# RWKV time mixing: inputs split once into two parts, wider weight splits, unmasked key products, factors padded to 112 rows

## The chip, the cores and the metric

One Trainium2 chip, of which the kernel uses one core. The core has TensorE (PE, with its weight loads shown apart as PEld), VectorE (DVE), ScalarE (ACT), GpSimd (POOL), SyncE (SP, which here only issues transfers) and 16 DMA engines. The metric is the device time of one execution in microseconds; the median of several runs counts.

## The reference

Two layers of a bidirectional encoder trunk, 256 tokens, width 2048, float32, one batch. Layer 0 is a Hyena/GLA block and an MLP, layer 1 an RWKV-7 block and an MLP; each sub-block has an adaLN in front and a gated residual behind. The change lies in the RWKV block alone:

```python
def rwkv7_block(h, mu, w_r, w_k, w_v, w0, w1, w2, a0, a1, a2, g1, g2, k_k, k_a, r_k, gn_g, gn_b, w_o):
    xx = 0.5 * (hp[:, :-2] + hp[:, 2:]) - h
    xr, xw, xk, xv, xa, xg = [h + xx * mu[j] for j in range(6)]
    r, k, v = heads(xr @ w_r), heads(xk @ w_k), heads(xv @ w_v)
    g = jax.nn.sigmoid(xg @ g1) @ g2
    kk = k * k_k;  kk = kk * rsqrt(max(sum(kk * kk), 1e-24))
    for d in range(2):                              # forwards and backwards
        logw = -0.606531 * sigmoid(w0[d] + tanh(xw @ w1[d]) @ w2[d])
        a = sigmoid(a0[d] + (xa @ a1[d]) @ a2[d])
        k_d = k * (1.0 + (a - 1.0) * k_a)
        # scan over time, per head (64 x 64 state):
        #   state = state * w_t + (state @ -kk_t) (kk_t * a_t)^T + v_t k_t^T;  o_t = state @ r_t
        state_out += o_d
        bonus += sum(r * k_d * r_k) * v
    o = groupnorm(state_out) * gn_g + gn_b + bonus
    return (o * g) @ w_o
```

The kernel does the scan in chunks of 64 tokens. Per head and chunk it needs the products of the decayed keys with each other, a 64x64 matrix `N`, and the inverse of a unit triangular matrix built from its strictly lower part.

## The kernel before

All large products are made of three TensorE products: each float32 operand is split into a high part (a cast to the type fp32r, on ACT) and a low part (the operand less its high part), and hi·hi, hi·lo and lo·hi are added up (`prod`, lines 502 to 507). The split itself is `split`, line 465: a cast on ACT (L466) and a subtraction on DVE, or on POOL where that engine is named (both L467).

The RWKV block (label `tm`, function `rwkv`) runs in these stages.

The **mixing stage**: the normalized input `h` and its difference `xx` are in SBUF. `spill_mixes` (L1275) forms xk, xr and xv, two of 16 feature tiles at a time, as float32 and writes them to the DRAM tensors `mix2`, `mix0` and `mix3`. `lora` (L1284) beside it makes the low-rank inputs. The first key products run woven into this.

The **keys stage**: four groups `n` of eight heads. For each, `rwkv_linear` (L1021) streams k, then r: eight tiles of weights of 128x1024 (512 KB) and eight input tiles `xu` (256 KB) read back from DRAM. `stream` (L994) prepares one tile ahead: it loads `xu` (two buffers), splits it with ACT and POOL into `xh` and `xl`, loads the next weights and splits the present ones in two halves of 512 columns (`split_weights`, with `fine` 2 from the constants `W1`, `W2`), ACT for `wh`, DVE for `wl`. So each of the four groups of each of the three products loads and splits the same input anew: 96 tiles. Woven between is `rwkv_keys` (L1326) for each of 16 pairs of heads `p`, twice (`d`, the direction): it takes LoRA factors `up` (97 rows: 96 and a bias; one load of 97x1024 for two pairs, L1180), forms decays, exponentials and the tile `ab` (DVE, L1374 to L1377), the products `N` in PSUM (L1387), multiplies them with the mask `nm` on their way to SBUF (DVE, L1393) and stores `ab` and `N` to DRAM. `invert` (L1405) of the group before runs beside it: long rows of small DVE steps (L1421, L1422), which read the strictly lower triangle only.

The **values stage** and the **output product**: `pair_load`, `pair_prep`, `pair_chain` and `pair_tail` for each pair, woven with the v products of the groups 1 to 3 (through `stream` again) and the output product `rwkv_out`.

What sets the order: `weave` deals out steps of these generators in given proportions, and a scheduler with a timeline model then orders each engine's instructions; every engine works through its own row in order. All loads and stores of the RWKV block except three go through SP's single row. In the program a transfer also waits until the one eight before it, which had the same completion semaphore, has landed. The last third of the kernel, the second MLP, follows when the output product is done.

Of the kernel before, what the change touches and what calls it, by code (L numbers as in the profile page):

```python
# [9 lines left out]
F32 = mybir.dt.float32  # L10
F32R = mybir.dt.float32r
# [97 lines left out]
def _rwkv_constants():  # L109
    o = {}  # L110
    for d in range(2):
        st = _block_tri(64, True, d == 1)
        inc = _block_tri(64, False, d == 1)
        o[f"cum{d}"] = np.concatenate([st, inc], axis=1) * np.float32(-0.606531)
        st64, inc64 = st[:64, :64], inc[:64, :64]
        z = np.zeros((64, 64), np.float32)
        top = np.concatenate([z, inc64], axis=1)
        bot = np.concatenate([st64, inc64], axis=1)
        o[f"mm{d}"] = np.concatenate([bot, top] if d else [top, bot], axis=0)
    lower = np.tril(np.ones((64, 64), np.float32), -1)  # L120
    o["nm"] = np.concatenate([lower, lower], axis=0)
    h = np.arange(P) // 64
    o["bo"] = (h[:, None] == h[None, :]).astype(np.float32)
    return o


def layout(i):
# [56 lines left out]
    for n, v in _rwkv_constants().items():  # L184
        (rk1 if n[:3] in ("cum", "nm") else rk).add(n, v)
    a["rc"], a["rc1"] = rk.array(), rk1.array()
# [28 lines left out]
class Build:  # L215
# [21 lines left out]
    def run(self):  # L237
# [3 lines left out]
        self.due, self.rate, self.turn, self.hold, self.starting = 0.0, 0.0, 0, None, False  # L241
        self.cut = None
        self.small = self.pool(ctx, "small", bufs=2)
# [221 lines left out]
    def split(self, a, hi, lo, eng=None):  # L465
        self.nc.scalar.copy(hi, a)  # L466
        d = (eng or self.nc.vector).tensor_tensor(lo, a, hi, ALU.subtract)  # L467
# [20 lines left out]
    def load(self, name, n, i, pools):  # L488

        self.turn += 1  # L490
        w = self.t(pools[self.turn % len(pools)], [P, 2, NB], "w")
        self.dma = self.nc.sync.dma_start(w, self.A[name][n, i // 2][:, i % 2 * 2 : i % 2 * 2 + 2]).ins
        self.tick(self.rate / 2)
        return w
# [487 lines left out]

    def open_linear(self, st, bufs, fine, finex):
        self.fine, self.finex = fine, finex
        self.ws = self.pool(st, self.name("ws"), bufs=bufs, reuse_waits="tile")
# [8 lines left out]
    def stream(self, name, n, src, tiles):  # L994

        nc = self.nc
        w = [self.load(name, n, 0, [self.wp])]

        def ahead(i):
            u = self.t(self.xt, [P, 2, T], "xu", bufs=2)  # L1000
            nc.sync.dma_start(u, src[:, 2 * i : 2 * i + 2, :])
            x = [self.t(self.xt, [P, 2, T], t, dt=F32R) for t in ("xh", "xl")]
            for j in range(self.finex):
                c = slice(j * T // self.finex, (j + 1) * T // self.finex)
                self.split(u[:, :, c], *(a[:, :, c] for a in x), nc.gpsimd)
# [8 lines left out]
        for i in range(tiles // 2):  # L1014
# [3 lines left out]
            for k in range(2):  # L1018
                yield 2 * i + k, [a[:, k, :] for a in x], [a[:, k, :] for a in v]

# [79 lines left out]
    def rwkv(self):  # L1100
# [12 lines left out]
        with ExitStack() as st:  # L1113
# [35 lines left out]
            with ExitStack() as st2:  # L1149
# [11 lines left out]
                self.xstack.close()  # L1161
                self.rate = 0.0
                mixes = self.spill_mixes(h, xx)
# [5 lines left out]
            with st1:  # L1169
                p1 = self.pool(st1, "p1", reuse_waits="tile")  # L1170
                for n in range(4):
# [3 lines left out]
                    def lane(o):  # L1175
                        for i in range(2):
                            p = 4 * n + 2 * i + o
                            if o == 0:
                                up[i] = self.t(p1, [97, 4, T], "up", bufs=2)
                                nc.sync.dma_start(up[i], A["rw_up"][p // 2])  # L1180
# [9 lines left out]
            with ExitStack() as st1:  # L1190
                self.open_linear(st1, 2, W2, X2)
                p2 = self.pool(st1, "p2", reuse_waits="tile")
# [68 lines left out]
                for n in range(4):  # L1261
# [9 lines left out]
                    self.residual("tm", n, pts[n])  # L1271
        self.open_gate()
# [53 lines left out]
    def rwkv_keys(self, rp, p, r, k, kk, kh, up):  # L1326
# [11 lines left out]
        for d in range(2):  # L1338
# [16 lines left out]
            Gp.tensor_tensor(u[1 - d], sc, k, ALU.mult)
# [4 lines left out]
            en = self.t(rp, [P, T], "en", bufs=3)  # L1360
            pt = self.pt([P, 2, 2, P])
# [12 lines left out]
            V.tensor_tensor(ar[:, 0, :], ar[:, 0, :], kk, ALU.mult)  # L1374
            for n in range(2):
                V.tensor_tensor(bk[:, :, n, :], c4(u[n]), c4(en), ALU.mult)
            V.tensor_tensor(ar[:, 1, :], ar[:, 1, :], r, ALU.mult)  # L1377
# [14 lines left out]
            for hd in range(2):  # L1392
                V.tensor_tensor(nt[:, hd], pts[hd], self.rc("nm").unsqueeze(1).to_broadcast([P, 2, 64]), ALU.mult)  # L1393
            nc.sync.dma_start(self.nd[b][:, d, 256 * pb : 256 * pb + 256], nt.rearrange("p h t j -> p (h t j)"))
# [319 lines left out]
```

## Time and profile before

| | us |
|---|---|
| median of 3 runs (range) | 3164.84 (3163.99 to 3170.43) |
| the profiled execution, its own time | 3173.39 |
| its span, first to last instruction | 3171.6 |
| PE busy | 2904.6 (92%) |
| DVE busy | 2195.9 (69%) |
| ACT busy | 1340.4 (42%) |
| POOL busy | 620.7 (20%) |
| mean granted TensorE clock | 0.96 |

The strip of the page cuts the span in 40 slices of 79 us; each digit is a busy share in tenths:

```profile
PE   5999899999999999979577777999998999999998
DVE  7899776657777787787368685975556677555554
PEclk9999999999999999999788897998999999999999
```

Slices 18 to 30 are the RWKV block. Read a time on the page with two things in mind. Matmuls are pipelined, so that the durations of a group add up to more than the stretch in which they ran; the busy time of a stretch counts overlaps once. And an idle engine costs only where the work that ends last hangs on it: a wait is to be followed to what ended it.

### The profile page before, as it was taken

The numbers are of one execution on the slowest core, as the hardware profiler recorded it, in microseconds if no ns is written. First come the engines' busy times: TensorE is split into PE (matmuls) and PEld (weight loads), VectorE is DVE, ScalarE is ACT, GpSimd is POOL, SyncE is SP. The second block draws the span as 40 slices with busy tenths as digits, with TensorE's granted clock in tenths as the row PEclk, the third lists the DMA queues.
The fourth block names the chain that finished last, engine by engine and source line by source line (L and its number), as shares of the span: only waits on it lengthen the run. The fifth ranks groups of instructions, "written<-read, shape, count | busy, mean of one in ns | idle before, by whom it ended". The sixth has DMA issues, their size and how long they took to land. (4 is left out here: it accounts for less than half of the span.)

```text
span 3171.6 us, 52610 instructions
## 1 busy us (share of the span) xinstructions
PE 2904.6 (92%) x20308; PEld 2513.1 (79%) x20308; DVE 2195.9 (69%) x3350; ACT 1340.4 (42%) x2083; POOL 620.7 (20%) x646
## 2 busy tenths in 40 slices
PE   5999899999999999979577777999998999999998
PEld 2677776799988998868476676787777998899986
DVE  7899776657777787787368685975556677555554
ACT  3233444444433444433354553444445444344443
POOL 1211100021100110023355464442323110001100
PEclk9999999999999999999788897998999999999999
DMA  9978777648889888966455567896635678555552
GB/s 320 326 257 290 245 269 265 230 150 285 291 305 314 291 295 301 311 214 226 152 185 175 178 208 192 270 292 208 192 108 192 224 250 284 196 188 180 199 193 99
DMA packets 285494, 741.39 MB, mean 234 GB/s; under 512 B 73601, under 2 KB 100097, under 8 KB 284092
## 3 DMA queue, kind: packets, MB, share of 16 engines
q1 hardware_dynamic: 284668, 734.40, 69.0%
q8 instruction: 159, 2.61, 0.3%
q10 hardware_dynamic: 576, 3.64, 0.3%
q14 instruction: 91, 0.75, 0.1%
HBM read 697.23 MB, written 40.70 MB: 233 GB/s over the span
## 5 line engine op out<-in xcount | busy, mean ns | idle before, releaser
L467 DVE TENSOR_TENSOR f_wl<-f_w,f_wh 128x1024 fp32r<-128x1024 f32 x512 | 631.0, 1233 | 444.5 <-ACT f_wh L466 440.4
L466 ACT CAST f_wh<-f_w 128x1024 fp32r<-128x1024 f32 x512 | 538.4, 1052 | 748.3 <-PE f_mm L507 319.3
L506 PE MATMUL f_mm<-f_h,f_wh 128*128 128x256 f32 x2048 | 579.6, 283 | 0.0
L505 PE MATMUL f_mm<-f_h,f_wh 128*128 128x256 f32 x2048 | 579.4, 283 | 0.0
L507 PE MATMUL f_mm<-f_h,f_wl 128*128 128x256 f32 x2048 | 579.0, 283 | 0.0
L506 PE MATMUL f_mm<-f_wl,f_hid 128*128 128x512 f32 x1024 | 398.6, 389 | 0.6 <-DVE f_wl L467 0.6
L507 PE MATMUL f_mm<-f_wh,f_hid 128*128 128x512 f32 x1024 | 398.5, 389 | 0.0
L506 PEld LDWEIGHTS f_mm<-f_h,f_wh 128*128 128x128 f32 x2048 | 393.2, 192 | 0.2
L505 PEld LDWEIGHTS f_mm<-f_h,f_wh 128*128 128x128 f32 x2048 | 393.0, 192 | 0.1
L507 PEld LDWEIGHTS f_mm<-f_h,f_wl 128*128 128x128 f32 x2048 | 392.9, 192 | 0.0
L505 PE MATMUL f_mm<-f_wh,f_hid 128*128 128x512 f32 x1024 | 357.9, 389 | 0.0
L467 POOL TENSOR_TENSOR f_hid<-f_u,f_hid 128x512 fp32r<-128x512 f32 x64 | 98.0, 1531 | 990.0 <-ACT f_hid L466 985.2
L467 DVE TENSOR_TENSOR tm_wl<-tm_w,tm_wh 128x512 fp32r<-128x512 f32 x256 | 206.0, 830 | 99.0 <-ACT tm_wh L466 98.4
L363 DVE SCALAR_TENSOR_TENSOR mix_w<-mix_w,mix_s 128x1024 f32<-128x1024 f32 x175 | 219.8, 1265 | 73.3 <-DMA mix_w<-in_ada_f 49.1
L505 PE MATMUL tm_mm<-tm_xh,tm_wh 128*128 128x256 f32 x768 | 242.9, 320 | 18.5 <-ACT tm_xh L466 11.1
L506 PE MATMUL tm_mm<-tm_xl,tm_wh 128*128 128x256 f32 x768 | 234.5, 306 | 8.8 <-POOL tm_xl L467 8.8
L363 DVE SCALAR_TENSOR_TENSOR f_w<-f_w,mix_s 128x1024 f32<-128x1024 f32 x174 | 233.4, 1344 | 2.3 <-DMA f_w<-in_ada_f 2.3
L507 PE MATMUL tm_mm<-tm_xh,tm_wl 128*128 128x256 f32 x768 | 232.6, 305 | 1.4 <-DVE tm_wl L467 1.4
L467 POOL TENSOR_TENSOR tm_xl<-tm_xu,tm_xh 128x512 fp32r<-128x512 f32 x113 | 169.4, 1500 | 310.5 <-ACT tm_xh L466 268.8
L506 PEld LDWEIGHTS f_mm<-f_wl,f_hid 128*128 128x128 f32 x1024 | 192.2, 188 | 40.9 <-DVE f_wl L467 1.2
L507 PEld LDWEIGHTS f_mm<-f_wh,f_hid 128*128 128x128 f32 x1024 | 192.2, 188 | 39.8
L505 PEld LDWEIGHTS f_mm<-f_wh,f_hid 128*128 128x128 f32 x1024 | 192.3, 188 | 39.7
(445 smaller groups left out, 5413.9 us busy)
## 6 DMA issues: line engine op xcount, KB each, us to landing
f_w<-in_w SPq DMA_DIRECT2D x512, 512.0 KB, 4.9
f_w<-in_ada_f SPq DMA_DIRECT2D x125, 512.0 KB, 5.5
mix_w<-in_ada_mix SPq DMA_DIRECT2D x96, 512.0 KB, 6.4
mix_w<-in_w_in SPq DMA_DIRECT2D x80, 512.0 KB, 5.2
mix_w<-in_ada_f SPq DMA_DIRECT2D x64, 512.0 KB, 5.0
f_w<-in_ada_tm SPq DMA_DIRECT2D x49, 512.0 KB, 5.7
tm_xu<-mix SPq DMA_DIRECT2D x96, 256.0 KB, 4.8
mix_w<-in_w_out SPq DMA_DIRECT2D x32, 512.0 KB, 4.7
```

The source lines that it names most:

```text
L363: V.scalar_tensor_tensor(w, w, 1.0, self.s[:, j * (D // 2) : (j + 1) * (D // 2)], ALU.mult, ALU.mult, accum_out=a[:, j, i : i + 1])
L466: self.nc.scalar.copy(hi, a)
L467: d = (eng or self.nc.vector).tensor_tensor(lo, a, hi, ALU.subtract)
L505: mm(out, lhsT=l[0], rhs=r[0], start=start, stop=False)
L506: mm(out, lhsT=l[0], rhs=r[1], start=False, stop=False)
L507: mm(out, lhsT=l[1], rhs=r[0], start=False, stop=stop)
```

## The change

- `spill_mixes` splits each mixed tile at once, with ACT and POOL: 24 splits for 96. The parts of xk stay in SBUF, in two tiles `xk` of 128x8x2x256 in fp32r. The parts of xr and xv go to DRAM as one tensor each, 512 KB per two feature tiles (16 stores of 512 KB for 24 of 256 KB), through two buffers `xs`.
- `stream` takes a slice of `xk` for the keys, and for r and v loads both parts in one transfer straight to the matmuls' operand (64 loads of 512 KB for 96 of 256 KB; three buffers). It loads weights three tiles ahead (`PF`).
- `W1` and `W2` go from 2 to 1: a weight tile is split by one cast and one subtraction of 1024 columns.
- `N` is copied from PSUM by ACT and no longer masked by DVE; the mask leaves the constants. The triangle that is read later is the same.
- The two DVE products of `bk` become one of 128x512, with `u` as one tile; `th` and `en` have two buffers for three.
- `rw_up` gets 15 rows of zeros, 112 in all; the matmuls use 97 as before.
- `wq` and `casts` are new names for another queue of weights; `wq` is None throughout, so nothing runs through them.

```diff
-W1, W2, X1, X2 = 2, 2, 1, 1
+W1, W2 = 1, 1
-PK = 8
+PK, PF = 8, 3
...
-    a["rw_up"] = np.stack(up, axis=1).reshape(97, 4, 8, T).transpose(2, 0, 1, 3)
+    up = np.stack(up, axis=1).reshape(97, 4, 8, T).transpose(2, 0, 1, 3)
+    a["rw_up"] = np.concatenate([up, np.zeros((8, 15, 4, T), np.float32)], axis=1)
...
     def stream(self, name, n, src, tiles):
         nc = self.nc
-        w = [self.load(name, n, 0, [self.wp])]
+        w = [self.load(name, n, i, [self.wp]) for i in range(PF)]
         def ahead(i):
-            u = self.t(self.xt, [P, 2, T], "xu", bufs=2)
-            nc.sync.dma_start(u, src[:, 2 * i : 2 * i + 2, :])
-            x = [self.t(self.xt, [P, 2, T], t, dt=F32R) for t in ("xh", "xl")]
-            for j in range(self.finex):
-                c = slice(j * T // self.finex, (j + 1) * T // self.finex)
-                self.split(u[:, :, c], *(a[:, :, c] for a in x), nc.gpsimd)
-            if 2 * i + 2 < tiles:
-                w.append(self.load(name, n, i + 1, [self.wp]))
+            if isinstance(src, list):
+                x = src[i // 4][:, 2 * i % 8 : 2 * i % 8 + 2]
+            else:
+                x = self.t(self.xt, [P, 2, 2, T], "x", bufs=self.xb, dt=F32R)
+                nc.sync.dma_start(x.bitcast(F32), src[:, 2 * i : 2 * i + 2])
+            if 2 * (i + PF) < tiles:
+                w.append(self.load(name, n, i + PF, [self.wp]))
             v = [self.t(self.ws, [P, 2, NB], t, dt=F32R) for t in ("wh", "wl")]
             self.split_weights(w[i], v)
             return x, v
...
-        self.xd = {j: tc.dram_tile([P, KT, T], F32, name=f"mix{j}") for j in (0, 2, 3)}
+        self.xd = {j: tc.dram_tile([P, KT, 2, T], F32, name=f"mix{j}") for j in (0, 3)}
...
+            xk = self.pool(st1, "xk", reuse_waits="tile")
+            self.xd[2] = [self.t(xk, [P, 8, 2, T], f"xk{i}", dt=F32R) for i in range(2)]
...
     def spill_mixes(self, h, xx):
...
-                self.nc.sync.dma_start(self.xd[j][:, k : k + 2, :], u)
+                if j == 2:
+                    x = self.xd[2][k // 8][:, k % 8 : k % 8 + 2]
+                else:
+                    x = self.t(self.hp, [P, 2, 2, T], "xs", bufs=2, dt=F32R)
+                self.split(u, x[:, :, 0], x[:, :, 1], self.nc.gpsimd)
+                if j != 2:
+                    self.nc.sync.dma_start(self.xd[j][:, k : k + 2], x.bitcast(F32))
...
-                                up[i] = self.t(p1, [97, 4, T], "up", bufs=2)
+                                up[i] = self.t(p1, [112, 4, T], "up", bufs=2)
...
-            for n in range(2):
-                V.tensor_tensor(bk[:, :, n, :], c4(u[n]), c4(en), ALU.mult)
+            V.tensor_tensor(bk, u.rearrange("p n (c t) -> p c n t", t=64), c4(en).unsqueeze(2).to_broadcast([P, 4, 2, 64]), ALU.mult)
...
-                V.tensor_tensor(nt[:, hd], pts[hd], self.rc("nm").unsqueeze(1).to_broadcast([P, 2, 64]), ALU.mult)
+                S.copy(nt[:, hd], pts[hd])
```

Every engine's order up to the RWKV block is the one of before. Three places within it follow, first as before, then as changed.

SP's row around the fourth load of factors, in group 1 of the keys stage (`xu` and `x` are inputs read back from `mix`, `w` weights, `E` the input of the inversion, `N` and `ab` stores of the keys):

```order
846 L1394 DMA nd_11803<-tm_N_13713 128x256
847 L1001 DMA tm_xu_13880<-mix_11783 128x512
848 L1180 DMA tm_up_14625<-in_rw_up 97x1024
849 L1001 DMA tm_xu_13994<-mix_11784 128x512
850 L1413 DMA tm_E_14020<-nd_11803 16x32x32 x4
851 L492 DMA tm_w_14266<-in_rw_k 128x1024
852 L1001 DMA tm_xu_14077<-mix_11784 128x512
853 L1402 DMA ab_11789<-tm_bon_13519 128x264
854 L1394 DMA nd_11803<-tm_N_13936 128x256
```

```order
819 L1009 DMA tm_x_13704<-mix_11783 128x1024
820 L494 DMA tm_w_13810<-in_rw_k 128x1024
821 L494 DMA tm_w_13884<-in_rw_k 128x1024
822 L1406 DMA nd_11802<-tm_N_13559 128x256
823 L1186 DMA tm_up_14365<-in_rw_up 112x1024
824 L1009 DMA tm_x_14140<-mix_11783 128x1024
825 L1425 DMA tm_E_13828<-nd_11802 16x32x32 x4
826 L494 DMA tm_w_13923<-in_rw_k 128x1024
```

Before, each weight tile has an `xu` load beside it, the keys' too. In the change the `x` loads here belong to r; the keys' stream has weights only, and they are issued three tiles ahead.

ACT's row in the keys stage (`wh`, `xh` are casts, `sig`, `th`, `sc`, `ab`, `en` steps of `rwkv_keys`):

```order
836 L466 CAST tm_wh_14385<-tm_w_14375 128x512 x2
837 L466 CAST tm_xh_14379<-tm_xu_14377 128x512
838 L1364 ACTIVATE tm_ab_14360<-tm_ps_14362 128x2x2x128
839 L1365 ACTIVATE tm_en_14361<-tm_ps_14362 128x256
840 L466 CAST tm_wh_14428<-tm_w_14333 128x512 x2
841 L466 CAST tm_xh_14424<-tm_xu_14422 128x512
842 L1343 ACTIVATE tm_sig_14406<-tm_ps_14407 128x256
```

```order
820 L465 CAST tm_wh_13925<-tm_w_13672 128x1024
821 L1377 ACTIVATE tm_ab_13876<-tm_ps_13878 128x2x2x128
822 L1378 ACTIVATE tm_en_13877<-tm_ps_13878 128x256
823 L465 CAST tm_wh_13999<-tm_w_13810 128x1024
824 L1356 ACTIVATE tm_sig_13948<-tm_mm_13949 128x256
825 L1361 ACTIVATE tm_th_13954<-tm_ps_13955 128x256
826 L1363 ACTIVATE tm_sc_13958<-tm_th_13954,tm_ksc_11818 128x256
827 L465 CAST tm_wh_14040<-tm_w_13884 128x1024
828 L1405 COPY tm_N_13975<-tm_ps_13976 128x128
829 L1405 COPY tm_N_13975<-tm_ps_13981 128x128
```

The casts of inputs are gone from the stage, a weight tile has one cast, and the copies of `N` stand among them.

DVE's row in the keys stage (`z` and `T` are the inversion's steps):

```order
1471 L1393 TENSOR_TENSOR tm_N_15084<-tm_ps_15085,tm_rc_1977_11836 128x128
1472 L1393 TENSOR_TENSOR tm_N_15084<-tm_ps_15090,tm_rc_1977_11836 128x128
1473 L1374 TENSOR_TENSOR tm_ab_15008<-tm_ab_15008,tm_kk_13447 128x256
1474 L1376 TENSOR_TENSOR tm_ab_15008<-tm_u_2672_15004,tm_en_15009 128x4x64
1475 L1376 TENSOR_TENSOR tm_ab_15008<-tm_u_2673_15005,tm_en_15009 128x4x64
1476 L1421 TENSOR_TENSOR tm_z_15043<-tm_E_14020,tm_T_14029 128x87
```

```order
1321 L466 TENSOR_TENSOR tm_wl_14041<-tm_w_13884,tm_wh_14040 128x1024
1322 L1434 TENSOR_TENSOR tm_T_13837<-tm_T_13837,tm_z_13917 128x29x3
1323 L1387 TENSOR_TENSOR tm_ab_13989<-tm_ab_13989,tm_kk_13321 128x256
1324 L1389 TENSOR_TENSOR tm_ab_13989<-tm_ab_13989,tm_r_12736 128x256
1325 L1388 TENSOR_TENSOR tm_ab_13989<-tm_u_2402_13986,tm_en_13990 128x512
1326 L1433 TENSOR_TENSOR tm_z_13941<-tm_E_13828,tm_T_13837 128x112
```

The masks are gone, and the two products of 4x64 are one of 512.

More of the change, by code (lines that the diff above doesn't have):

```diff
@@ L184, in layout @@
     for n, v in _rwkv_constants().items():
-        (rk1 if n[:3] in ("cum", "nm") else rk).add(n, v)
+        (rk1 if n[:3] == "cum" else rk).add(n, v)
     a["rc"], a["rc1"] = rk.array(), rk1.array()
@@ L241, in run @@
         self.due, self.rate, self.turn, self.hold, self.starting = 0.0, 0.0, 0, None, False
-        self.cut = None
+        self.cut, self.casts, self.wq = None, [], None
         self.small = self.pool(ctx, "small", bufs=2)
@@ L465, in split @@
     def split(self, a, hi, lo, eng=None):
-        self.nc.scalar.copy(hi, a)
+        c = self.nc.scalar.copy(hi, a)
         d = (eng or self.nc.vector).tensor_tensor(lo, a, hi, ALU.subtract)
@@ L469, in split @@
             self.cut = d.ins
+            self.casts = [c.ins]
     def behind(self):
@@ L491, in load @@
         w = self.t(pools[self.turn % len(pools)], [P, 2, NB], "w")
-        self.dma = self.nc.sync.dma_start(w, self.A[name][n, i // 2][:, i % 2 * 2 : i % 2 * 2 + 2]).ins
+        src = self.A[name][n, i // 2][:, i % 2 * 2 : i % 2 * 2 + 2]
+        if self.wq is None:
+            self.dma = self.nc.sync.dma_start(w, src).ins
+        else:
+            with self.tc.issue_after(self.casts[-1]):
+                self.wq.dma_start(w, src)
         self.tick(self.rate / 2)
@@ L981, in mixed, with open_linear @@
         self.nc.vector.scalar_tensor_tensor(o, xx[k // 8][:, k % 8, :], self.v(f"mu{j}")[:, k : k + 1], h[k // 8][:, k % 8, :], ALU.mult, ALU.add)
-    def open_linear(self, st, bufs, fine, finex):
-        self.fine, self.finex = fine, finex
+    def open_linear(self, st, bufs, fine, xb):
+        self.fine, self.xb = fine, xb
         self.ws = self.pool(st, self.name("ws"), bufs=bufs, reuse_waits="tile")
@@ L1018, in stream @@
             for k in range(2):
-                yield 2 * i + k, [a[:, k, :] for a in x], [a[:, k, :] for a in v]
+                yield 2 * i + k, [x[:, k, a] for a in range(2)], [a[:, k, :] for a in v]
     def rwkv_linear(self, name, n, j, out):
@@ L1161, in rwkv @@
                 self.xstack.close()
-                self.rate = 0.0
+                self.rate, self.wq = 0.0, None
                 mixes = self.spill_mixes(h, xx)
@@ L1178, in lane @@
                             if o == 0:
-                                up[i] = self.t(p1, [97, 4, T], "up", bufs=2)
+                                up[i] = self.t(p1, [112, 4, T], "up", bufs=2)
                                 nc.sync.dma_start(up[i], A["rw_up"][p // 2])
                             c = p % 4
-                            yield from self.rwkv_keys(p1, p, r[:, c, :], k[:, c, :], kk[:, c, :], kh[:, c, :], up[i][:, :, o * P : (o + 1) * P])
+                            yield from self.rwkv_keys(p1, p, r[:, c, :], k[:, c, :], kk[:, c, :], kh[:, c, :], up[i][:97, :, o * P : (o + 1) * P])
                     def late():
@@ L1190, in rwkv @@
             with ExitStack() as st1:
-                self.open_linear(st1, 2, W2, X2)
+                self.open_linear(st1, 2, W2, 3)
                 p2 = self.pool(st1, "p2", reuse_waits="tile")
@@ L1271, in rwkv @@
                     self.residual("tm", n, pts[n])
+        self.wq = None
         self.open_gate()
@@ L1344, in rwkv_keys @@
             Gp.tensor_scalar(sig, sig, 0.5, 0.5, ALU.mult, ALU.add)
-            th = self.t(rp, [P, T], "th", bufs=3)
+            th = self.t(rp, [P, T], "th", bufs=2)
             pt = self.pt([P, T])
@@ L1352, in rwkv_keys @@
             yield 1
-            u = [self.t(rp, [P, T], f"u{n}", bufs=3) for n in range(2)]
-            V.scalar_tensor_tensor(u[d], th, 1.0, kh, ALU.add, ALU.mult)
-            Gp.tensor_tensor(u[1 - d], sc, k, ALU.mult)
+            u = self.t(rp, [P, 2, T], "u2", bufs=3)
+            V.scalar_tensor_tensor(u[:, d], th, 1.0, kh, ALU.add, ALU.mult)
+            Gp.tensor_tensor(u[:, 1 - d], sc, k, ALU.mult)
             ab = self.t(rp, [P, 1024], "ab", bufs=4)
```

7 lines of the change are left out of this document (3 added, 4 removed).

## The prediction

> **What bounds the kernel now.** I first read the strip of forty slices: TensorE (PE) is at 9 tenths nearly everywhere except between the two MLPs, where the RWKV layer runs. There I took the busy times by stage, on the stages that the code gives.
>
> ```profile
> 1400.00:1500.00 100.00, 89.74 (x554) 78.69 (x555) 77.56 (x130) 34.12 (x58) 38.47 (x29) 0.97 0.66 222
> 1500.00:1960.00 460.00, 325.76 (x2475) 292.93 (x2475) 304.73 (x575) 212.56 (x426) 224.87 (x279) 0.83 0.56 181
> 1960.00:2190.00 230.00, 224.35 (x2555) 187.61 (x2553) 172.43 (x386) 97.89 (x249) 88.88 (x106) 0.93 0.88 263
> 2190.00:2400.00 210.00, 206.30 (x2342) 157.16 (x2341) 121.72 (x273) 99.49 (x255) 58.75 (x91) 1.00 0.52 157
> ```
>
> Columns: stretch, its length, busy us (and instructions) of PE, weight loads, DVE, ACT and POOL, the granted clock, the DMA share, GB/s. The first row is the stage that mixes the inputs, the second the **keys stage**, the third the values, the fourth the output product. In the other three PE is 90 to 98% busy: there is next to nothing to win. In the keys stage no engine is: PE 326 of 460, DVE 305, and the clock is down to 0.83. PE idles 460 − 326 = 134 us there, so this stage decides. The waits of that stage, by what ended them (us in total, times, longest):
>
> ```profile
> ACT tm_xh L466 <- DMA tm_xu<-mix: 129.6, 28, 14.9
> PE tm_ps L1387 <- DVE tm_ab L1376: 40.2, 13, 6.6
> PE tm_ps L1317 <- ACT tm_u L1315: 23.9, 3, 10.5
> PE tm_mm L505 <- ACT tm_xh L466: 5.9, 2, 3.2
> PE tm_mm L506 <- POOL tm_xl L467: 4.2, 3, 2.9
> ```
>
> ACT stands 130 us before the cast of an input tile that has not landed, and as ACT works in order, everything behind it (weights' casts, exponentials, evacuations) stands too. PE rarely waits for the tile itself (10 us), but for what is late behind it. The long ones of ACT's waits, and one more of the same origin, one by one:
>
> ```profile
> 1525.82 0.38 ACT L1343 ACTIVATE tm_sig<-tm_ps 128x256 f32<-128x256 f32 x1 [15.24 <-PE tm_ps L1342]
> 1545.04 0.62 ACT L466 CAST tm_xh<-tm_xu 128x512 fp32r<-128x512 f32 x1 [14.88 <-DMA tm_xu<-mix]
> 1584.39 0.62 ACT L466 CAST tm_xh<-tm_xu 128x512 fp32r<-128x512 f32 x1 [12.82 <-DMA tm_xu<-mix]
> 1637.30 0.62 ACT L466 CAST tm_xh<-tm_xu 128x512 fp32r<-128x512 f32 x1 [13.95 <-DMA tm_xu<-mix]
> 1694.55 0.62 ACT L466 CAST tm_xh<-tm_xu 128x512 fp32r<-128x512 f32 x1 [10.45 <-DMA tm_xu<-mix]
> 1750.25 0.62 ACT L466 CAST tm_xh<-tm_xu 128x512 fp32r<-128x512 f32 x1 [9.11 <-DMA tm_xu<-mix]
> 1805.42 0.62 ACT L466 CAST tm_xh<-tm_xu 128x512 fp32r<-128x512 f32 x1 [9.08 <-DMA tm_xu<-mix]
> 1860.05 0.62 ACT L466 CAST tm_xh<-tm_xu 128x512 fp32r<-128x512 f32 x1 [13.79 <-DMA tm_xu<-mix]
> ```
>
> They come every 55 us, that is once for each load of LoRA factors (`up`, eight in all), and add up to 99.3 us. What such a load does is seen where the first two are issued, on the SP queue and in the DMA view of the 12 us behind them:
>
> ```profile
> 1505.26 5.37 SPq L1180 DMA_DIRECT2D tm_up<-in_rw_up  x2
> 1510.73 14.68 SPq L492 DMA_DIRECT2D tm_w<-in_rw_k  x1
> ...
> DMA packets 78, 0.32 MB, mean 26 GB/s; under 512 B 1, under 2 KB 1, under 8 KB 78
> q1 hardware_dynamic: 78, 0.32, 6.4%
> ```
>
> 6.4% of sixteen engines is one engine. The 97-row load, 388 KB, runs on a single DMA engine at 26 GB/s: 14.9 us each. Every other transfer needs its share of that engine too, so all that is issued behind it lands late (the weights' load issued at 1510 after 32 us), and SP itself holds its next issue for 14.7 us.
>
> **The change, part by part.** Profiled execution: 3173.4 us, 8.6 above the median of the three runs (3164.84), so I subtract 8.6 at the end.
>
> (a) **Factors of 112 rows.** The load grows to 448 KB; no row shows 112 rows. The nearest loads have 128 rows and 512 KB:
>
> ```profile
> tm_w<-in_rw_r SPq DMA_DIRECT2D x24, 512.0 KB, 8.1
> tm_w<-in_rw_k SPq DMA_DIRECT2D x22, 512.0 KB, 5.3
> ```
>
> So 5 to 8 us if it spreads as these do, and 448 / 26 = 17 us if it stays on one engine. I take 5.3: 112 is sixteen times seven, 97 is prime, and one engine for 97 rows is what a division into equal shares would give. The Trainium skill's page DMA: Bandwidth & Descriptors (section Why a DMA increments its semaphore by 16 and not by 1) has that rule: a transfer gets the largest number of engines up to 16 that divides its outermost sizes. The 6.4% agrees for 97; for 112 it gives all sixteen, which no run here shows yet, and by the opposite the sum would be that of the fourth case below.
> What goes is at most the 99.3 us less one load that is still waited for at the start, 94. At least it is PE's own idle time around these loads: eight waits of PE, from 14.94 to 3.22 us, 67.0 in all; the first and the last of them:
>
> ```profile
> 1524.59 1.19 PE L1342 MATMUL tm_ps<-tm_up,tm_hw 97*128 97x128 f32 x4 [14.94 <-DMA tm_up<-in_rw_up]
> 1850.53 0.37 PE L1387 MATMUL tm_ps<-tm_ab 64*64 64x64 f32 x2 [6.04 <-DVE tm_ab L1376]
> ```
>
> I take **−85**, nearer the upper end, because after such a gap the clock is low (0.83 in the mean) and goes up where the gaps go.
>
> (b) **Inputs split once.** In the keys stage the casts and subtractions of inputs go, and with them the other 129.6 − 84.1 = 45.5 us (21 short waits) of ACT's for them. The costs of this and the next edits:
>
> ```profile
> L466 ACT CAST tm_xh<-tm_xu 128x512 fp32r<-128x512 f32 x59 | 36.6, 620 | 136.3 <-DMA tm_xu<-mix 129.6 <-PE tm_mm L507 3.7 <-POOL tm_kr L1398 3.0
> L467 POOL TENSOR_TENSOR tm_xl<-tm_xu,tm_xh 128x512 fp32r<-128x512 f32 x58 | 88.6, 1530 | 151.8 <-ACT tm_xh L466 133.9 <-issue 15.3 <-DMA ab<-tm_ab 2.5
> L467 DVE TENSOR_TENSOR tm_wl<-tm_w,tm_wh 128x512 fp32r<-128x512 f32 x122 | 102.8, 866 | 69.1 <-ACT tm_wh L466 69.0
> L467 DVE TENSOR_TENSOR f_wl<-f_w,f_wh 128x1024 fp32r<-128x1024 f32 x512 | 631.0, 1233 | 444.5 <-ACT f_wh L466 440.4
> L466 ACT CAST f_wh<-f_w 128x1024 fp32r<-128x1024 f32 x512 | 538.4, 1052 | 748.3 <-PE f_mm L507 319.3
> L466 ACT CAST tm_wh<-tm_w 128x512 fp32r<-128x512 f32 x120 | 68.3, 620 | 18.4 <-PE tm_mm L506 18.1
> L1376 DVE TENSOR_TENSOR tm_ab<-tm_u,tm_en 128x256 f32<-128x256 f32 x64 | 33.2, 554 | 2.4 <-POOL tm_u L1355 2.4
> L1393 DVE TENSOR_TENSOR tm_N<-tm_ps,tm_rc 128x128 f32<-128x128 f32 x48 | 12.8, 280 | 7.4 <-PE tm_ps L1387 6.4 <-PE tm_mm L1387 1.0
> L1551 ACT COPY tm_R<-tm_ps 128x128 f32<-128x128 f32 x26 | 6.7, 264 | 14.7 <-PE tm_ps L1549 14.1 <-PE tm_ps L1523 0.4
> ```
>
> 59 casts (36.6 us) leave ACT, 58 subtractions (88.6) leave POOL; both have idle time, so only the waits count: between PE's own 10.1 us for these tiles and the 45.5 of ACT. The keys' parts are in SBUF, but r's and v's parts are waited for by PE instead, so I stay near PE's row: **−15**.
>
> (c) **Weights, key products, merged products.** DVE: 61 wide subtractions at 1.233 for 122 narrow ones, 75.2 − 102.8 = −27.6; 64 masks at 0.28, −17.9; 32 products of 512 for 64 of 256. The merged form isn't in the trace: not below the 554 ns of one half, not above two of them; at the 866 of a 128x512 operation 27.7 − 33.2 = −5.5. In all −51 of 305 us. ACT: −36.6, wide casts 60 × 1.052 − 68.3 = −5.2, and 64 copies from PSUM added at 264 ns (the R0 copies are of that shape), +16.9. The copies wait for products in ACT's in-order queue, ahead of the next weights' cast; DVE's wait there was 7.4 us, so that is the cost if ACT is no longer idle. DVE's saving counts only where DVE is full, as in
>
> ```profile
> 1650.00:1670.00 20.00, 17.65 (x157) 16.44 (x156) 18.56 (x41) 12.78 (x28) 12.83 (x17) 1.00 0.77 237
> 1710.00:1730.00 20.00, 15.98 (x121) 14.54 (x120) 20.00 (x31) 9.70 (x21) 15.47 (x12) 0.83 0.52 177
> ```
>
> Seven such pieces of 20 us at 87% or more: 140 us with one sixth less DVE work, about 23 of them. With something left to PE: **−20** (0 to −51).
>
> (d) **Mixing stage.** It gets 24 casts and 24 subtractions at once (15 + 37 us by the rows above, on engines 34 and 38% busy), less some 18 of each that it did before. Sixteen spills of 512 KB go through two buffers: cast 0.6, subtraction 1.5, and a landing, 2.1 as the spills now or 5.3 as the loads above,
>
> ```profile
> mix<-tm_u SPq DMA_DIRECT2D x20, 256.0 KB, 2.1
> ```
>
> so 4.2 to 7.4 us a round, eight rounds in 34 to 59 us of a stage of 100: hidden, unless SP holds the spill behind a load, and then ACT's cast of weights behind it waits. **+3** (−5 to +25).
>
> (e) **Values stage.** 24 input loads of 512 KB for 256: 6.3 MB more, 24 us at 263 GB/s, beside 12% idle DMA share of 230 us (28). It just fits. **+4** (−5 to +24). The reserve of three weight tiles costs nothing in the keys stage, since no adaLN load uses that pool there. The output product and the MLPs keep their order.
>
> Sum: −85 − 15 − 20 + 3 + 4 = **−113**; 3173.4 − 113 − 8.6 = **3052**. The keys stage would take 340 us, with PE at 326 or less at a better clock: close to PE's limit, so the parts cannot bring much more than I took.
>
> **Rivals.** *PE alone sets the keys stage.* If no wait is left and the clock is full, its work is 0.83 × 326 = 270 us; with 25 for the start and the seams 295, −165 instead of −120, no loss in (d), (e): 3173.4 − 165 − 8.6 = 3000. For it: all waits hang on few causes. Against: L1387 waits for DVE at every step, and DVE still has 254 us.
> *New waits take over.* Only PE's certain 67 go, and the norm's (L1317) and DVE's chains fill the rest: 3173.4 − 67 + 7 − 8.6 = 3105.
> *The 112 rows stay on one engine*, so the change does not do what it says in (a). Then (b) and (c) act alone, and the reserve of three weight tiles, some 16 us at 5.5 us a tile, hides nothing of the inputs: −35 + 7, 3137.
> *Slower: PE waits for parts.* What ACT waited for at a distance, PE now waits for directly, with no cast between that is run ahead. 64 loads of 512 KB are issued on SP behind stores that wait for DVE. A tile of parts has three buffers, so a lead of two units, some 11 us in the keys stage, against a landing of 5 to 8 plus the hold on SP. If each comes late by the 2.2 us of the present short waits (45.5 / 21), it is +141: 3173.4 − 113 + 141 − 8.6 = 3193. It decides from 113 / 64 = 1.8 us a load. Against: the lead covers the landing, and half the keys stage reads from SBUF.
>
> **How the numbers follow.** Forecast 0.60 (3020 to 3085), PE alone 0.18, new waits 0.13, one engine 0.04, slower 0.05. The range takes the bounds of (a), (b), (c) and both neighbours: **2995 to 3110**. A measurement of this kernel can tell 0.2% (6 us) from no change: faster 0.94, same 0.01, slower 0.05.
>
> **What would show it.** (a) right: no DMA stretch at 6% behind a factor load, SP's issues behind it under 3 us, none of ACT's 9 to 15 us waits, clock above 0.9 in the keys stage. (b): POOL's busy time there down by some 90 us, and PE's waits for parts under 15 us in all. (c): no slice with DVE full and PE starved. (d), (e): these stages within 5 us of their length. Wrong would be PE waits ended by the parts' DMA in the r streams, or the same gaps every 55 us.

## The result, and the profile after

| | before | after |
|---|---|---|
| median of 4 runs (range), us | 3166.76 (3163.99 to 3170.43) | 3045.84 (3041.96 to 3049.38) |
| profiled execution, us (span) | 3173.39 (3171.6) | 3047.34 (3045.3) |

The ratio is 0.9617 with an interval of 0.96 to 0.9634: 3.8% or 121 us faster. The forecast was 3052.

From the page of the changed kernel, busy times and strip:

```profile
PE 2871.4 (94%) x20308; PEld 2488.7 (82%) x20308; DVE 2122.1 (70%) x3126; ACT 1301.6 (43%) x1947; POOL 522.2 (17%) x574
...
PE   6999989999999999997999878999998999999998
...
DVE  7899866657777788787768875775646776455454
...
PEclk9999999999999999998999987999999999999999
```

DVE and POOL lost busy time (74 and 98 us), ACT some (39). To put the gain in its place, the two stages are cut at the same events in every kernel: the **keys stage** from the issue of the first `up` load to the last ACT copy of `bon`, the **values stage** from there to the last ACT copy of `v`. First the kernel before, then the changed one; columns: stretch, length, busy us (and instructions) of PE, weight loads, DVE, ACT and POOL, granted clock, DMA share, GB/s.

```profile
1505.30:1927.80 422.50, 297.71 (x2241) 268.55 (x2240) 285.36 (x540) 198.36 (x401) 211.73 (x256) 0.84 0.55 179
1927.80:2181.10 253.30, 238.65 (x2688) 200.92 (x2686) 180.79 (x398) 105.49 (x259) 99.62 (x125) 0.90 0.88 260
```

```profile
1508.60:1803.10 294.50, 261.88 (x2203) 239.83 (x2203) 227.54 (x395) 175.97 (x351) 135.81 (x197) 0.95 0.82 264
1803.10:2057.90 254.80, 232.64 (x2678) 195.75 (x2677) 170.42 (x365) 90.05 (x214) 62.23 (x103) 0.89 0.90 270
```

The prediction cut the keys stage wider, at 460 us; its differences compare, its lengths don't. The keys stage is 128 us shorter, which is more than the whole difference of the two executions (126). It starts 3 us later, and the values stage is 1.5 us longer. Inside the keys stage PE's idle time (length less busy) went from 124.8 to 32.6 us, and PE was busy 36 us less for nearly as many instructions (2203 for 2241), while the clock rose from 0.84 to 0.95 (297.7 x 0.84 / 0.95 is 263, measured 261.9). What is left of waits there, first ACT's, then PE's (us in total, times, longest):

```profile
ACT tm_wh L465 <- PE tm_mm L511: 29.2, 26, 3.0
ACT tm_N L1405 <- PE tm_mm L1399: 17.4, 7, 6.1
```

```profile
PE tm_ps L1399 <- DVE tm_ab L1388: 15.7, 10, 4.1
PE tm_ps L1376 <- POOL tm_sig L1357: 5.5, 5, 1.8
PE tm_mm L510 <- DMA tm_x<-mix: 3.0, 1, 3.0
```

The 130 us that ACT stood before input tiles are gone, with all waits of 9 to 15 us. Now ACT mostly waits for PE. PE's own longest group, for DVE's `ab`, fell from 40.2 us to 15.7.

SP's queue at the first pair of factor loads (start, us), and from the DMA view of the stage the eight loads with their median time to landing:

```profile
1508.57 0.91 SPq L1186 DMA_DIRECT2D tm_up<-in_rw_up  x2
1511.12 12.16 SPq L494 DMA_DIRECT2D tm_w<-in_rw_r  x4
...
tm_up<-in_rw_up SPq DMA_DIRECT2D x8, 448.0 KB, 8.2
```

The 448 KB land in 8.2 us, where one engine at 26 GB/s would take 17. The next issue isn't held for 14.7 us any more: four take 12.16.

### The profile page after: what moved, and what is told of

Same layout as the page of the kernel before. It is cut to its first block, busy times and chain, and to the rows that moved or that the text cites. A ratio compares the mean times of both kernels' runs of the same rounds, so it can differ in the third digit from the quotient of the medians.

```text
span 3045.3 us, 52042 instructions
## 1 busy us (share of the span) xinstructions
PE 2871.4 (94%) x20308; PEld 2488.7 (82%) x20308; DVE 2122.1 (70%) x3126; ACT 1301.6 (43%) x1947; POOL 522.2 (17%) x574
## 5 line engine op out<-in xcount | busy, mean ns | idle before, releaser
L466 DVE TENSOR_TENSOR f_wl<-f_w,f_wh 128x1024 fp32r<-128x1024 f32 x512 | 630.8, 1233 | 444.3 <-ACT f_wh L465 433.4
L466 DVE TENSOR_TENSOR tm_wl<-tm_w,tm_wh 128x1024 fp32r<-128x1024 f32 x128 | 164.4, 1287 | 85.8 <-ACT tm_wh L465 81.6
L465 ACT CAST mix_wh<-mix_w 128x1024 fp32r<-128x1024 f32 x114 | 119.4, 1050 | 201.2 <-PE mix_mm L512 86.3
L510 PE MATMUL tm_mm<-tm_x,tm_wh 128*128 128x256 f32 x512 | 161.2, 316 | 12.3 <-DMA tm_x<-mix 10.8
L465 ACT CAST tm_wh<-tm_w 128x1024 fp32r<-128x1024 f32 x128 | 133.4, 1046 | 86.7 <-PE tm_mm L511 60.3
L466 DVE TENSOR_TENSOR mix_wl<-mix_w,mix_wh 128x1024 fp32r<-128x1024 f32 x114 | 142.4, 1254 | 38.8 <-ACT mix_wh L465 38.7
```

The lines of the kernel that those rows point to most:

```text
L465: c = self.nc.scalar.copy(hi, a)
L510: mm(out, lhsT=l[0], rhs=r[0], start=start, stop=False)
```

## The experiments

Twelve kernels were measured in four sets, each beside the kernel before, whose median was 3174.1, 3169.5, 3170.9 and 3170.3 us in them. So kernels of different sets are compared by their ratios to before; 0.01 of ratio is 32 us. Three kernels put one part of the change into the kernel before and one puts two; two more set the dose of (a) there. Five take one part out of the changed kernel, and one gives it 98 rows of factors.

### The rows of the factor load, in the kernel before

Only the array and the tile are padded, with zeros; the matmuls use 97 rows throughout. n is 98, 106 or 112:

```diff
-    a["rw_up"] = np.stack(up, axis=1).reshape(97, 4, 8, T).transpose(2, 0, 1, 3)
+    up = np.stack(up, axis=1).reshape(97, 4, 8, T).transpose(2, 0, 1, 3)
+    a["rw_up"] = np.concatenate([up, np.zeros((8, n - 97, 4, T), np.float32)], axis=1)
...
-                                up[i] = self.t(p1, [97, 4, T], "up", bufs=2)
+                                up[i] = self.t(p1, [n, 4, T], "up", bufs=2)
```

With 98 rows every engine's order is that of before, with 106 all but two rows on PE; with 112 the scheduler orders some later instructions otherwise.

> The kernel before with one edit: a row of zeros is added to the factors, 98 rows for 97; every engine's order is the one of before. Theory of the one engine (a load of 97 rows runs on one DMA engine, 14.9 us at 26 GB/s, and holds up all that is behind it): 98 is 14 times 7, so 14 engines carry it, about 1.1 us each; ACT's seven waits of 9 to 15 us for inputs and the one at the start go, the time falls by 67 to 94 us, to 3072 to 3098, and the clock in the keys stage goes above 0.88. Rival (multiples of 16 alone spread, or the gain of 112 rows comes from another order of instructions): 98 rows change nothing, 3160 to 3170, and a DMA share of 6% stays behind each load. Rival (the inputs' splitting in ACT's row is what holds the stage, so other waits of ACT take over): 3130 to 3155.

> The kernel before with 106 rows of factors (9 of zeros) and every engine's order as before. 106 is twice 53: by the theory of the one engine two engines carry it, 212 KB each, 8.2 us at 26 GB/s per engine, and what was 14.9 us of hold per load becomes about 8: of 85 us some 35 to 55 go, 3110 to 3130. Rival (only the number of rows or the multiple of 16 counts): 3160 to 3170, as before, or as with 98 rows, 3072 to 3098.

> The kernel before with the 112 rows of the change alone (the scheduler orders some later instructions otherwise). Theory of the one engine: within 15 us of 98 rows, 3065 to 3105, so that this part alone gives 67 to 94 of the change's 121 us. Rival (the gain needs the inputs split once, since ACT still waits for them): 3130 to 3155.

Measured: 98 rows 3085.80 us, ratio 0.9719 (0.9703 to 0.9734), 106 rows 3114.44, 0.981 (0.9788 to 0.9831), 112 rows 3110.83, 0.9796 (0.9779 to 0.9814). SP's queue at the first pair of factor loads and behind it (start, us), with 106 rows and with 98:

```profile
1507.88 0.98 SPq L1181 DMA_DIRECT2D tm_up<-in_rw_up  x2
1508.96 5.85 SPq L493 DMA_DIRECT2D tm_w<-in_rw_k  x1
```

```profile
1506.38 1.25 SPq L1181 DMA_DIRECT2D tm_up<-in_rw_up  x2
1507.73 0.47 SPq L493 DMA_DIRECT2D tm_w<-in_rw_k  x1
```

The hold of the next issue is 14.68 us with 97 rows, 5.85 with 106, 0.47 with 98. 97 is prime, 106 is 2 x 53, 98 is 14 x 7: one, two and fourteen equal shares. The keys stage follows (98, 106, 112 rows; of the first and the last the values stage too):

```profile
1506.40:1848.40 342.00, 280.86 (x2242) 257.39 (x2242) 294.48 (x540) 199.04 (x401) 213.17 (x256) 0.91 0.70 221
1848.40:2093.70 245.30, 230.60 (x2688) 194.27 (x2686) 180.62 (x398) 105.26 (x259) 98.79 (x125) 0.94 0.89 263
```

```profile
1507.90:1876.30 368.40, 284.86 (x2241) 259.07 (x2241) 289.18 (x540) 198.30 (x401) 208.97 (x256) 0.89 0.64 206
```

```profile
1506.90:1854.40 347.50, 283.64 (x2250) 259.69 (x2249) 294.99 (x546) 199.36 (x404) 215.12 (x256) 0.90 0.70 220
1854.40:2120.40 266.00, 238.27 (x2693) 199.67 (x2693) 180.82 (x394) 104.36 (x259) 92.98 (x125) 0.90 0.84 249
```

With 97, 106 and 98 rows the stage takes 422, 368 and 342 us: it follows the dose. One row of zeros takes 2.8% off the kernel. The Trainium skill's rule that the prediction weighed (page DMA: Bandwidth & Descriptors, section Why a DMA increments its semaphore by 16 and not by 1: the largest number of engines up to 16 that divides the outermost sizes) gives 1, 2, 14 and 16 engines here. Holds and stages follow it for 97, 106 and 98 rows; the numbers 14 and 16 themselves are counted in no row, but the 8.2 us above fit 16. That a multiple of 16, or another order, made the gain is ruled out by 98 rows.

The 112 rows missed their range by 6 us. In the keys stage they lose 5 us against 98 rows, in the values stage 21, at a lower clock (0.90 for 0.94), with nearly the same instructions there (2693 for 2688 on PE). More on this below.

### 97 and 98 rows in the changed kernel

> The changed kernel with the factors back at 97 rows (the scheduler orders some instructions of the RWKV block otherwise). Theory of the one engine: the holds come back, at most 8 times 14.9 us; with inputs resident for the keys and weights three tiles ahead part of each is hidden, so the time rises by 40 to 85 us, to 3085 to 3130. Rival (the reserve of three tiles hides the hold, the inputs were the cause): up by under 20 us, 3045 to 3065.

> The changed kernel with 98 rows of factors for 112 (14 engines by the dose seen in the kernel before, one row of zeros). By the theory of the engines within 12 us of the changed kernel, 3034 to 3058, and some 70 to 80 us below the one with 97 rows, though its schedule differs from both; the keys stage 290 to 305 us. If the 77 us of the 97 rows in the changed kernel were for the most part its other schedule, this kernel, which also has one, stands 30 us or more above the changed one.

Measured: 97 rows 3123.66 us, 0.9864 (0.984 to 0.9888); 98 rows 3046.08, 0.9605 (0.9581 to 0.963), the same as the changed kernel though its order differs. So the 0.0247 (78 us) that 97 rows cost here are the load's, not the schedule's. The keys stage is 367.0 us long with 97 rows and 287.7 with 98. What PE waits for with 97 rows in it, the longest groups:

```profile
PE tm_mm L509 <- DMA tm_x<-mix: 39.6, 4, 16.0
PE tm_ps L1398 <- DVE tm_ab L1387: 19.2, 12, 4.9
PE tm_ps L1354 <- DMA tm_up<-in_rw_up: 12.2, 1, 12.2
```

The first row is four waits for the parts of r's inputs, up to 16 us. Before, PE hardly ever waited for such a tile itself; with no cast between, it does, where something holds the DMA.

### Inputs split once, in the kernel before

The diff of `spill_mixes` and `stream` above, with `PF` 3 and two buffers of `th` and `en`, and 97 rows, narrow weights and masks as before.

> The kernel before with the inputs split once (keys' parts in SBUF, the others in DRAM as parts, weights three tiles ahead, two buffers for th and en), with 97 rows, weights split 512 wide, masks and two products as before. Theory of the one engine: the holds of 14.9 us stay, and only the short waits go: 15 to 45 us, 3120 to 3150; ACT's long waits turn into waits of ACT, DVE or PE for weights. Rival (the inputs hold the stage): 70 to 110 us go, 3055 to 3095, since keys' inputs are resident and three weight tiles cover the hold.

Measured: 3128.03 us, 0.9857 (0.9834 to 0.9879), -46 us. This edit brings the costs (d) and (e) of the prediction with it, so by its terms -15 + 3 + 4 = -8 us was to come. The keys stage:

```profile
1518.80:1879.80 361.00, 268.10 (x2183) 246.06 (x2182) 243.00 (x534) 167.63 (x340) 127.22 (x209) 0.87 0.64 209
```

It is 61.5 us shorter, four times the term of (b); it starts 13.5 us later, and the values stage is 6.8 us longer (260.1). POOL has 84.5 us less, about as forecast. But DVE, from which this edit takes nothing, has 42.4 us less with all but six of its instructions (their number is in brackets). Its weight subtractions, first in the kernel before, then here (busy, mean ns):

```profile
L467 DVE TENSOR_TENSOR tm_wl<-tm_w,tm_wh 128x512 fp32r<-128x512 f32 x112 | 95.1, 873 | 63.4 <-ACT tm_wh L466 63.4
```

```profile
L467 DVE TENSOR_TENSOR tm_wl<-tm_w,tm_wh 128x512 fp32r<-128x512 f32 x107 | 81.2, 779 | 15.8 <-ACT tm_wh L466 15.6
```

These rows are 14 of the 42 us, some 4 of them for five subtractions fewer. Why each took longer is seen in the timeline of the kernel before, at two places where both engines subtract, and at one where POOL does alone (start, us):

```profile
1661.37 1.28 DVE L467 TENSOR_TENSOR tm_wl<-tm_w,tm_wh 128x512 fp32r<-128x512 f32 x2
1661.89 2.14 POOL L467 TENSOR_TENSOR tm_xl<-tm_xu,tm_xh 128x512 fp32r<-128x512 f32 x1 [2.51 <-ACT tm_xh L466]
...
1675.40 2.37 DVE L467 TENSOR_TENSOR tm_wl<-tm_w,tm_wh 128x512 fp32r<-128x512 f32 x2
1675.64 1.58 POOL L467 TENSOR_TENSOR tm_xl<-tm_xu,tm_xh 128x512 fp32r<-128x512 f32 x1 [1.09 <-ACT tm_xh L466]
...
1641.63 1.27 POOL L467 TENSOR_TENSOR tm_xl<-tm_xu,tm_xh 128x512 fp32r<-128x512 f32 x1
```

Undisturbed, a pair of DVE's halves takes 1.28 us and POOL's subtraction 1.27. At 1661 DVE has its usual time and POOL takes 0.87 longer; at 1675 DVE takes 1.09 longer and POOL 0.31. One stands while the other works. The Trainium skill has the rule (page SBUF — State Buffer, section SBUF: two separate sides): DVE with two SBUF inputs and a GpSimd instruction that reads SBUF share one pair of ports, held whole by one instruction at a time. The rows agree.

The whole 42 us can be counted in the traces. Take each DVE instruction of the keys stage with the busy time that it adds, and compare it with the median of those of its own group and shape that meet no POOL instruction. In the kernel before, the 224 that meet none are 1 us above it in all, the 107 that meet an `xl` subtraction 45 us, the 209 that meet only other work of POOL 35 us. With the inputs split once these are 3, 0 and 39 us: the `xl` subtractions held DVE up by 40 to 45 us. The 64 masks, which read one of their two inputs from PSUM, take 0.28 us with POOL at work (40 of them) and without (24), as that rule has it. So a subtraction on POOL is not off DVE's account.

What it was worth to PE is seen in its waits for DVE's `ab`. In the kernel before the prediction shows a group of 40.2 us, and this is the second; behind it those of this kernel, with the wait that came instead:

```profile
PE tm_mm L1387 <- DVE tm_ab L1376: 16.3, 3, 11.5
```

```profile
PE tm_mm L505 <- DMA tm_x<-mix: 33.9, 5, 13.7
PE tm_ps L1394 <- DVE tm_ab L1383: 20.2, 10, 4.5
PE tm_mm L1394 <- DVE tm_ab L1383: 9.4, 1, 9.4
```

They fall from 56.5 to 29.6 us. The holds of the 97 rows are still there, and PE now meets them directly.

### Inputs split anew, and weights one tile ahead, in the changed kernel

First `stream` and `spill_mixes` as before (inputs loaded and split for each group, weights one ahead), the rest as changed; then only the reserve of weights undone:

```diff
-PK, PF = 8, 3
+PK, PF = 8, 1
```

> The changed kernel with the inputs spilled as float32 and split anew for each group, weights one tile ahead, as before; 112 rows, wide weight splits, unmasked products and merged products stay. My terms: 15 us of the short waits come back, and the subtractions on POOL (some 89 us) and casts on ACT (37) with them, which were not counted otherwise: 3055 to 3070. Rival (the inputs are worth their whole 45 us of ACT's short waits): 3085 to 3100.

> The changed kernel with the weights of r, k and v loaded one tile ahead instead of three; the inputs stay split once, 112 rows. It parts what undoing (b) cost (+54 us over the changed kernel) into the weights' reserve and the splits themselves. If the splits and their waits are the cost (ACT's and POOL's work, inputs that wait for a cast), this kernel stands within 10 us of the changed one: 3040 to 3056. If the reserve of weights is the greater part, 3070 to 3100, with ACT's casts L465 waiting for weights from DRAM in the keys stage. My recorded reading gave the reserve nothing in the keys stage.

Measured: splits undone 3100.42 us, 0.9779 (0.9754 to 0.9804), 0.0162 or 51 us over the changed kernel: the rival's range. Reserve alone undone 3059.07, 0.9648 (0.9617 to 0.968), 0.0031 or 10 us over it, and the intervals overlap. The second lies between the two ranges named for it. So the splits carry the greater part. The keys stage with splits undone, and a row of DVE on which nothing was edited, there and in the changed kernel:

```profile
1506.70:1849.60 342.90, 285.04 (x2237) 259.75 (x2236) 270.59 (x397) 207.71 (x409) 231.07 (x256) 0.89 0.71 222
...
L1360 DVE SCALAR_TENSOR_TENSOR tm_u<-tm_th,tm_rn 128x256 f32<-128x256 f32 x32 | 22.4, 702 | 14.8 <-ACT tm_th L1354 14.8
```

```profile
L1367 DVE SCALAR_TENSOR_TENSOR tm_u<-tm_th,tm_rn 128x256 f32<-128x256 f32 x32 | 17.4, 545 | 10.4 <-ACT tm_th L1361 10.4
```

Again 43.1 us of DVE (270.59 against 227.54) come and go with POOL's subtractions; counted as above, the DVE instructions that meet one are 50 us over their undisturbed time. The stage is 48.4 us longer: PE idles 57.9 us for 32.6, and is busy 23 longer at a clock of 0.89. Without the reserve the keys stage is 4 us longer than in the changed kernel (298.2) and the values stage 16 (270.8). PE idles there 25 us for 22, so the greater part isn't a wait for weights; that stage's own spread is taken up below.

### Wide weights, unmasked and merged products

In the kernel before, alone and with 98 rows (the two have the same order on every engine); `N` holds unmasked products, of which the inversion reads the lower triangle:

```diff
-W1, W2, X1, X2 = 2, 2, 1, 1
+W1, W2, X1, X2 = 1, 1, 1, 1
...
-            for n in range(2):
-                V.tensor_tensor(bk[:, :, n, :], c4(u[n]), c4(en), ALU.mult)
+            V.tensor_tensor(bk, u.rearrange("p n (c t) -> p c n t", t=64), c4(en).unsqueeze(2).to_broadcast([P, 4, 2, 64]), ALU.mult)
...
-                V.tensor_tensor(nt[:, hd], pts[hd], self.rc("nm").unsqueeze(1).to_broadcast([P, 2, 64]), ALU.mult)
+                S.copy(nt[:, hd], pts[hd])
```

> The kernel before with part (c) alone: weights split 1024 wide, N copied by ACT unmasked, merged products; 97 rows, inputs split anew per group. If DVE's work had a price of its own beside the factor loads, -20 of the sum: 3140 to 3162 beside 3170 for the kernel before. If ACT's waits for inputs behind the one-engine loads set the stage whatever DVE does, and ACT has the 64 copies more in its row, within 8 us of the kernel before: 3162 to 3178.

> Part (c) and 98 rows of factors together, in the kernel before; every engine's order is that of the kernel with (c) alone, which was 1.0049 of the time before. The theory that (c) pays as soon as the one-engine loads are gone: 10 to 30 us below the kernel with 98 rows alone (3086 us, 0.9719), so 3055 to 3076. The rival, that (c) takes from DVE but gives ACT, which still casts the inputs anew in the keys stage, 64 copies that wait for products, so that (c) pays only where those casts have left ACT: 3080 to 3105, and ACT's waits before L1392 copies and DVE's for L466 casts larger than with 98 rows alone.

Measured: alone 3185.95 us, 1.0049 (1.0033 to 1.0066), slower by 15 us; with 98 rows 3096.72, 0.9769 (0.9749 to 0.979), again 0.005 (16 us) above 98 rows alone. Neither theory had a loss alone; the second time lies in the rival's range. The keys stage with part (c) alone, then with 98 rows and part (c):

```profile
1509.30:1942.00 432.70, 296.52 (x2241) 267.76 (x2240) 266.18 (x397) 206.75 (x409) 223.64 (x256) 0.83 0.54 174
```

```profile
1502.40:1845.70 343.30, 282.89 (x2245) 257.65 (x2244) 274.50 (x397) 208.20 (x408) 227.70 (x256) 0.91 0.71 220
```

Alone, (c) makes the stage 10 us longer (432.7 for 422.5) though DVE has 19 us less. With 98 rows DVE has 20 us less than with 98 rows alone, and the stage is as long (343.3 for 342.0); the 16 us are lost in the values stage (262.6 for 245.3), so the rival's reason, ACT's copies in the keys stage, isn't shown: they wait 11.5 us there, and DVE's wait for casts is 15.2 for 13.8. PE's waits, with 98 rows alone and with (c):

```profile
PE tm_ps L1388 <- DVE tm_ab L1377: 37.9, 13, 8.7
PE tm_mm L1388 <- DVE tm_ab L1377: 4.2, 1, 4.2
PE tm_mm L1364 <- POOL tm_sig L1345: 3.7, 3, 1.9
PE tm_mm L508 <- DVE tm_wl L468: 2.8, 2, 2.1
```

```profile
PE tm_ps L1387 <- DVE tm_ab L1376: 20.0, 11, 3.9
PE tm_mm L507 <- POOL tm_xl L468: 8.6, 4, 4.9
PE tm_mm L1364 <- POOL tm_sig L1345: 8.5, 3, 3.6
PE tm_mm L508 <- DVE tm_wl L468: 7.0, 4, 2.7
PE tm_mm L1387 <- DVE tm_ab L1376: 5.3, 3, 2.7
```

The waits for `ab` fall from 42.1 to 25.3 us, and waits for POOL's `xl` and `sig` and for the now undivided `wl` take their place (24.1 for 6.5 in the rows shown). PE's idle time is the same, 60.4 for 61.1 us: the gain is turned into other waits.

Then the same parts undone in the changed kernel: weights in two halves (`W1, W2 = 2, 2`), and the mask back on DVE with its constant.

> The changed kernel with weights split in two halves of 512 columns. DVE gets 27.6 us more in the keys stage and ACT 5. My term is a part of 20 us: 8 to 15 us slower, 3054 to 3061. Rival (halves let the first products start earlier, and DVE has slack now, 236 of 315 us): 3040 to 3048.

> The changed kernel with the key products masked by DVE again instead of copied by ACT. DVE gets 18 us more, ACT 17 less in the keys stage. My term is a part of 20 us: 4 to 10 us slower, 3050 to 3056. Rival (ACT's in-order wait for the products, 26 us in the changed kernel, costs as much as DVE saves): within 3 us, 3043 to 3049, or faster.

Measured: halves 3058.05 us, 0.9651 (0.9628 to 0.9673), 11 us over the changed kernel (the intervals overlap by a little); mask 3065.25, 0.9669 (0.9655 to 0.9683), 16 over it, clear of noise. The first lies in the range of my term, the second above both of its ranges. By stages they don't confirm the reason: with halves the keys stage is 7 us *shorter* (287.1) and starts 12 later, with the mask it is 6 longer (300.1); the rest is in the values stages, 263.2 and 268.7 for 254.8, in which DVE's busy time is 3 us more with either edit (173.6 for 170.4). The one of the mask:

```profile
1808.60:2077.30 268.70, 245.93 (x2685) 206.76 (x2686) 173.62 (x385) 92.37 (x215) 60.89 (x99) 0.85 0.86 258
```

The clock is 0.85 for 0.89, PE is busy 13 us longer with as many instructions. Over all fourteen kernels this stage took 245 to 271 us, always nearly the same products: every edit in the keys stage makes the scheduler order what follows otherwise. But two kernels of one order differ too (253.3 before, 245.3 with 98 rows), with the same idle time of PE (14.7 us) at clocks of 0.90 and 0.94. What grants the higher clock there stays open, and so does every difference below that spread.

## Why the prediction was right, and where it wasn't

The time and the place were right: 3046 against 3052, and the keys stage at -128 us for the -120 of parts (a) to (c). Of the three large terms below that sum one was right; (b) was too small and (c) not borne out, and the two errors nearly cancelled. So the closeness of 3052 is in part luck.

- **(a), -85: right.** Alone, with the order kept, 2.81% or 88 us (98 rows); taken out of the changed kernel, 78. The split of the estimate holds as well: PE's idle time in the keys stage fell by 63.7 us (124.8 to 61.1), against the 67.0 counted from PE's eight waits, and PE was busy 16.9 less as the clock went from 0.84 to 0.91. The case of 112 rows on one engine is out. That 112 rows alone gave only 63 us lies mostly in the values stage.
- **(b), -15: too small by far.** In the keys stage -61.5 us, four times the term; the whole kernel with this part -46, where the terms (b), (d) and (e) add up to -8; 51 lost when undone. The step that failed is "both have idle time, so only the waits count": it took the 88.6 us of POOL's subtractions as free, as POOL idles. They held DVE up by 40 to 45 us, and DVE's `ab` is what PE waited for (56.5 us, 29.6 without them). How much of the gain is this, and how much the casts and waits that left ACT's row, these runs don't part. Even the upper end of the range given (45) was below what the keys stage lost.
- **(c), -20: not borne out; in the kernel before it costs 15 us alone and 16 beside 98 rows.** Row by row the terms look right: wide subtractions -26.3 us (76.1 for 102.4; forecast -27.6), masks -17, products -5.2 (28.9 for 34.1; -5.5). But DVE's total fell by 20, not by 51. The forecast set a mean that holds waits for POOL (866 ns a half) against one of the MLPs (1233), where 437 of 512 subtractions meet no POOL instruction. In the keys stage with 98 rows, undisturbed, a half takes 0.68 us (25 of 112) and with (c) a wide one 1.22 (9 of 56): 0.15 us a tile is saved, some 8 of the 26.3. The rest was waiting for POOL, and 16 us of it turn up at the other DVE instructions. And the 20 us that were left bought nothing, because PE's waits moved to POOL and `wl`. That a sixth of DVE's work in the pieces where it is full turns into time was the step that failed. Whether (c) earns its place in the changed kernel (11 and 16 us when a part is undone) isn't shown by the stages that it touches.
- **(d), +3: right** (the keys stage starts 3.3 us later). But two other kernels with these splits started it 13 to 15 us later than before, so the range was not too wide, and that it came to 3 here isn't explained.
- **(e), +4: not contradicted** (+1.5, and the DMA share 0.90), but the stage's spread of 26 us over the kernels is larger than the term. That the reserve of weights costs nothing in the keys stage held (4 us without it); the 16 us of the values stage without it are no more than that stage's spread.

From the side of before the parts add up if (a) is taken with 98 rows: -2.81 - 1.43 + 0.49 = -3.75% of 3170, -119 us, for -3.83% measured. With the 112 rows that the change has they don't: -2.04 - 1.43 + 0.49 = -2.98%, -94 us, and in the changed kernel 98 and 112 rows are the same. From the other side the parts come to 78 + 51 + 11 + 16 = 156 us for 121. So the sizes of single parts are good to some 25 us, the spread of the values stage.

Of the signs named ahead: no ACT wait is over 6.1 us, the clock is 0.95, PE waits 3.0 us for parts in the keys stage, POOL has 76 us less there (90 forecast), the other stages are within 5 us. Two fell short: the four issues behind the first factor loads still take 3.0 us each (12.16 in all), just over the limit named, and DVE is still nearly full in some pieces of 20 us where PE isn't (from 1710 to 1730 us DVE is busy 19.80 of 20 us, PE 18.11).

Of the rivals, "PE alone" came closest in the keys stage, but its full clock and its 165 us did not come. "PE waits for parts" fell as a whole, but its mechanism is real: it is what the changed kernel does with 97 rows, 39.6 us of it, and the kernel before with the inputs split once, 33.9.

## What to carry to other kernels

Look at the DMA view of the microseconds behind every load whose outer size splits into few equal shares (97 and 106 rows here): a share of 6.4% was one engine of sixteen, and the price is paid mostly by what is queued behind the load. Work moved to an idle POOL is not free while DVE is busy: compare the duration of the same DVE instruction where POOL works and where it doesn't, and take only undisturbed ones for a forecast. And where several engines of a stage are each some 60 to 85% busy, busy time saved on one of them may only move the waits to the next, as (c) did here; the removal of the 14.7 us holds, which started the chain, shortened the stage.

## What the runs showed of the hardware that was not expected

DVE and POOL subtractions of 128x512 that meet take turns: a pair of DVE's went from 1.28 us to 2.37, one of POOL's from 1.27 to 2.14. In sum the 56 of POOL's in the keys stage held DVE up by 40 to 45 us. DVE masks of 128x128 with one input in PSUM took 0.28 us either way. A load of 97 rows held the next issue of its queue for 14.7 us, one of 98 for 0.5. And in the keys stage the clock went with the gaps: with 97, 106 and 98 rows in the same order PE idled 125, 84 and 61 us at clocks of 0.84, 0.89 and 0.91, and from the first to the last the same instructions were busy 17 us less. In the values stage it did not: 14.7 us of idle time came with 0.90 and with 0.94.
